# Retention with its output feature-major, its steps between the next pair's projections, and TensorE in program order there

## The chip, the cores and the metric

One core of a Trainium2 chip runs the kernel. The metric is the device time of one execution in microseconds (us); three runs of the kernel before took 2668.18, 2663.58 and 2665.60 us, median 2665.6. A core has five engines with queues of their own: TensorE (PE, with its weight loads PEld), VectorE (DVE), ScalarE (ACT), GpSimd (POOL) and SyncE (SP), which issues most transfers.

## The reference

A backbone of two layers over 512 latent and 256 context tokens of width 1024, in float32. Each layer normalizes and modulates the tokens, projects them (`h @ w_in`) to queries, keys, values and gates, mixes tokens in three branches (window attention, a Fourier transform, retention), sums the branches by gates, projects, and runs 32 experts of which each token uses two. The change concerns retention, 8 heads of 64, chunks of 128 tokens, both directions:

```python
inner = jnp.einsum('bcihd,bcjhd->bchij', qc, kc) * dec[None, None]
o_inner = jnp.einsum('bchij,bcjhe->bcihe', inner, vc)
u = jnp.einsum('bcjhd,jh,bcjhe->bchde', kc, zeta, vc)
# s_prev: a scan over the chunks, s = g_chunk * s + u_c
o_cross = jnp.einsum('bcihd,ih,bchde->bcihe', qc, xi, s_prev)

def retention_out(o, g):                      # o: both directions' sum
    mu = jnp.mean(o, axis=-1, keepdims=True)
    var = jnp.mean(jnp.square(o - mu), axis=-1, keepdims=True)
    on = ((o - mu) * lax.rsqrt(var + GN_EPS)).reshape(B, T, RET_WIDTH)
    return (jax.nn.silu(g.astype(F32)) * on).astype(g.dtype)
```

## The kernel before, in words

The layers run one after the other; layer 0 computes latent and context tokens (6 tiles of 128), layer 1 writes the latent ones alone (4 tiles). `h` lies feature-major, each value split in a high and a low part. `proj` (L267) makes 128 features of all tokens: SyncE loads two tiles of weights `raw`, ScalarE and VectorE split them into `hl` (L237, L238), and TensorE does 24 matmuls of 512 moving columns for the latent tokens and 24 of 256 for the context (L275 to L277), into PSUM tiles `mm`. In layer 0 each `proj` ends with a step of the modulation of what comes later (`ada_step`: a 1 MB transfer `wada`, four matmuls L149 into the tile `ov`, VectorE's add L199).

Retention goes by pairs of heads p = 0 to 3. `ret_proj` makes k and q (each rotated by `rot`: VectorE L286, L287, GpSimd L288, L289), v (transposed to token-major `vtok` by `to_tokens`, L296) and the gate `sgr`. `ret_chain` makes token-major keys `ktok` (L296), values times decay (L444), q times decay (GpSimd, L438), the states (L452, then a recursion on VectorE), the inner products of keys and queries (L473, times the mask L475), and then the output of a tile of 128 tokens in token-major order, 64 features per head: L482 takes the masked products as stationary operand and v as moving one, L487 q as stationary and the state as moving one, 64 moving columns both. Mean, centred value and variance are VectorE reductions over the 64 features (L498 to L507) and ScalarE's square (L503), the inverse root is a power on GpSimd (L142), GpSimd multiplies (L509), TensorE transposes to feature-major (L514), and VectorE multiplies by the gate (L517) and splits (L243).

A scheduler chooses the order of each engine's instructions from the program, so retention's matmuls of a pair lie between those of the next pair's projections, or of the first of attention behind pair 3. PSUM tiles come from pools that set who waits: three banks `mm`, two `sc`, two `tr` (transposes), one `ov`. A stationary operand of type float32 takes two records of matmul in the trace.

Of the kernel before, what the change touches and what calls it, by code (L numbers as in the profile page):

```python
# [15 lines left out]
OP = mybir.AluOpType  # L16
# [18 lines left out]
T1_MASK, T1_KA, T1_VA = 0, 384, 1152  # L35
T2_LAT, T2_CTX, T2_CF, T2_ALT, T2_ALTC, T2_ROW, T2_ROWC, T2_N = 0, 1024, 1280, 1536, 1540, 1542, 1799, 1928
CP, _o = {}, 0
for _k, _n in (("ident", 128), ("tri", 128), ("iota1", 64), ("iota0", 32), ("i64", 16), ("kcon", 96), ("tok2", 6),
               ("hbm2", 2), ("zc", 2)):
    CP[_k] = (_o, _o + _n)  # L40
    _o += _n
# [19 lines left out]
def tile_backbone(ctx: ExitStack, tc: tile.TileContext, a: dict, out: bass.AP, stop=None, dbg=None):  # L61
# [51 lines left out]
    # DRAM scratch  # L113
# [6 lines left out]
    cin = const(16, "cin", a["c"])  # L120
    cp = const(480, "cp")
# [7 lines left out]
    tok2, hbm2, zc = (cp[:, CP[k][0]:CP[k][1]] for k in ("tok2", "hbm2", "zc"))  # L129
# [39 lines left out]
    def ada_feature(l, row):  # L169
        """sh1 and norm*(1+sc1), one value for each partition: [128, stream, kc]"""  # L170
# [21 lines left out]
    def ada_steps():  # L192
# [10 lines left out]
        # the last: over a partition's rows on DVE, over the partitions on PE (one stream, the latent one)  # L203
# [42 lines left out]
    def make_h(l, xt_l, xt_c):  # L246
        """xt_*: token-major tiles, already times rstd"""
# [70 lines left out]
    decay = {}  # L318

    def decay_logs(l):  # L320
# [13 lines left out]
        Z = cst.tile([128, 16], F32, name=f"Z{l}", tag="Z")      # [h of f | h of b]  # L334
# [26 lines left out]
    # =====================================================================  # L361
    def layer(l, xt_l, xt_c):
# [10 lines left out]
        rope, t1 = unit("rope"), unit("t1")  # L373
        SP.dma_start(rope, a["t1"][:, 0:2048])
        SP.dma_start(t1[:, 0:384], a["t1"][:, 2048:2432])
        CA, SA = rope[:, T1_CA:T1_CA + 512], rope[:, T1_SA:T1_SA + 512]
        CR, SR = rope[:, T1_CR:T1_CR + 512], rope[:, T1_SR:T1_SR + 512]
        mask = t1[:, T1_MASK:T1_MASK + 384]
# [10 lines left out]
        def o_tiles(b):  # L389
            """[high, low][group] of a branch's output, feature-major"""  # L390
# [10 lines left out]
        def ret_proj(p):  # L401
# [3 lines left out]
            sgr = rv[:, 768:1536]  # L405
            pc, pl = proj(l, p * 4, both)
# [10 lines left out]
            to_tokens(vtok, lambda i: (vc[:, i * 128:i * 128 + 128] if i < 2 else vl[:, (i - 2) * 128:(i - 1) * 128]),  # L417
                      ((0, 2), (2, 4)))
# [4 lines left out]
            return k, q, vtok, sgr  # L423

        def ret_chain(p, st):
            k, q, vtok, sgr = st
# [3 lines left out]
            vz = rb[:, 0:1536].rearrange("p (t h d e) -> p t h d e", t=6, h=2, d=2)  # L430
            St = rc[:, 0:768].rearrange("p (t d e) -> p t d e", t=6, d=2)
            ktok = rc[:, 768:1536].rearrange("p (t c) -> p t c", t=6)
            to_tokens(ktok, lambda i: k[:, i * 128:i * 128 + 128], ((0, 2), (2, 4)))
            # q times xi, for the states' part
            qs = slice(0, 768) if full else lsl
            nt = 6 if full else 4
            for d in range(2):
# [3 lines left out]
            for h in range(2):  # L441
                for d in range(2):
                    j = d * 8 + p * 2 + h
                    DVE.tensor_scalar(vz[:, :, h, d, :], vtok[:, :, h * 64:h * 64 + 64], Z[:, j:j + 1], None, op0=OP.mult)  # L444
            # states
            g_f, g_b = g128[:, p * 2:p * 2 + 1], g128[:, p * 2 + 1:p * 2 + 2]
            u = []
            for lo, n in ((0, 2), (2, 4)):
                up = pso()
                for i in range(n):  # L450
                    for h in range(2):
                        PE.matmul(up[h * 64:h * 64 + 64, i * 128:i * 128 + 128], ktok[:, lo + i, h * 64:h * 64 + 64],  # L452
                                  vz[:, lo + i, h, :, :], start=True, stop=True, skip_group_check=True)
# [12 lines left out]
            # inner products  # L466
            for lo, n in (((0, 2), (2, 4)) if full else ((2, 4),)):
                sc = [pss(), pss()]
                for i in range(n):
                    ts = slice((lo + i) * 128, (lo + i) * 128 + 128)  # L470
                    for h in range(2):
                        hs = slice(h * 64, h * 64 + 64)
                        PE.matmul(sc[h][:, i * 128:i * 128 + 128], k[hs, ts], q[hs, ts], start=True, stop=True)  # L473
                for h in range(2):
                    DVE.tensor_tensor(SD[:, h, lo:lo + n, :], sc[h][:, 0:n * 128].rearrange("p (t i) -> p t i", t=n),  # L475
                                      bmid(Dt[:, p * 2 + h, :], n), op=OP.mult)
            oo = [pss(), pss()]
            for t in TL:
                ts = slice(t * 128, t * 128 + 128)
# [909 lines left out]
```

## Time and profile before

| | |
|---|---|
| median of three runs | 2665.6 us |
| span of the profiled execution (first to last instruction) | 2652.4 us |
| mean granted clock of TensorE | 0.945 of full speed |
| TensorE busy | 2404.5 us, 91% |
| VectorE, ScalarE, GpSimd busy | 1045.9, 571.0, 469.6 us |
| moved by DMA | 594 MB, 224 GB/s on average |

The profiled execution's own time is its span with what lies around it at start and end; against the runs' median that is 13 us. A row of the timeline gives the start of a merged group of instructions, its busy time, the engine and line, the tiles written and read, their shape and number, and in brackets the idle time before it with what ended it. "PEclk" is the granted clock of TensorE over a stretch, 1.00 being 2.4 GHz. `sc`, `tr`, `ov` and `mm` are PSUM tiles; `ra` holds k and q, `rv` v and the gate, `rb` products and output, `rc` states and keys, `rq` q times decay.

### The profile page before, as it was taken

To read this page: it belongs to the slowest core of one execution; us is meant where nothing else is said; L and a number is where in the kernel's file an instruction comes from. 1 tells how busy PE (TensorE), PEld (TensorE's weight loads), DVE (VectorE), ACT (ScalarE), POOL (GpSimd) and SP (SyncE) were. 2 spreads that over 40 slices of the span, in tenths; PEclk is the share of its full clock that TensorE was granted. 3 is DMA by queue.
4 is the path that set the end of the run, shared out by engine and by line. 5 is a ranking of instruction groups with operands and counts; after the bars stand their busy time and mean duration, and the time that the engine had idled before them with its cause. 6 is when DMAs were issued, how large, how long until landed. Compare 5 with 4: busy or idle time off the path is not lost. (4 is left out here: it accounts for less than half of the span.)

```text
span 2652.4 us, 44021 instructions
## 1 busy us (share of the span) xinstructions
PE 2404.5 (91%) x17245; PEld 1580.7 (60%) x17245; DVE 1045.9 (39%) x3181; ACT 571.0 (22%) x1285; POOL 469.6 (18%) x414
## 2 busy tenths in 40 slices
PE   5999999999999979999999599999999898997774
PEld 3777766688889944434443388766888743343221
DVE  5434445635234643233332644565335521221112
ACT  3211134521223211011110422245224200000000
POOL 0212110000222412111211123210022321121111
PEclk8988889999999979999999799999999899998897
DMA  7423211235225389899999621110235599999996
GB/s 273 162 96 108 102 51 63 81 111 209 71 64 179 138 331 417 352 371 389 415 417 411 237 72 46 58 48 21 88 97 173 207 379 417 411 410 407 416 415 253
DMA packets 129730, 594.43 MB, mean 224 GB/s; under 512 B 20940, under 2 KB 22052, under 8 KB 73968
## 3 DMA queue, kind: packets, MB, share of 16 engines
q1 hardware_dynamic: 115184, 561.92, 55.0%
q0 software_dynamic: 13376, 26.27, 2.6%
q8 instruction: 138, 2.26, 0.3%
q10 hardware_dynamic: 960, 3.39, 0.3%
q14 instruction: 72, 0.59, 0.1%
HBM read 579.74 MB, written 28.25 MB: 229 GB/s over the span
## 5 line engine op out<-in xcount | busy, mean ns | idle before, releaser
L1079 PE MATMUL mm<-w_gu,xT 128*32 128x256 f32 (+1 forms) x3776 | 564.4, 505 | 85.1 <-DMA w_gu<-in_w_gu_dram 81.7
L1079 PEld LDWEIGHTS mm<-w_gu,xT 128*32 128x32 f32 (+1 forms) x3776 | 192.0, 127 | 390.8 <-issue 227.4
L275 PE MATMUL mm<-hH,hl 128*128 128x512 f32 x800 | 319.7, 401 | 1.7 <-DVE shuf L287 0.9
L276 PE MATMUL mm<-hL,hl 128*128 128x512 f32 x800 | 316.1, 395 | 0.0
L277 PE MATMUL mm<-hH,hl 128*128 128x512 f32 x800 | 315.5, 395 | 0.4 <-DVE hl L238 0.4
L238 DVE TENSOR_TENSOR hl<-raw,hl 128x512 fp32r<-128x512 f32 x248 | 183.3, 741 | 252.1 <-ACT hl L237 251.8
L1104 PE MATMUL mm<-w_d,aT 128*32 128x256 f32 (+1 forms) x1888 | 267.0, 488 | 6.9 <-DVE aT L1094 5.9
L237 ACT CAST hl<-raw 128x512 fp32r<-128x512 f32 x248 | 153.4, 620 | 385.9 <-PE mm L277 250.6
L1084 ACT ACTIVATE act<-mm 128x256 f32<-128x256 f32 (+1 forms) x87 | 30.1, 346 | 899.0 <-PE mm L1079 865.0
L1113 POOL DMA_INDIRECT y_d<-y,gd x87 | 87.7, 1008 | 742.3 <-DVE y L1112 562.3
L1104 PEld LDWEIGHTS mm<-w_d,aT 128*32 128x32 f32 (+1 forms) x1888 | 90.6, 124 | 157.0 <-issue 124.0
L1085 DVE TENSOR_TENSOR act<-act,mm 128x256 f32<-128x256 f32 (+1 forms) x87 | 32.2, 370 | 380.3 <-ACT act L1084 380.3
L275 PEld LDWEIGHTS mm<-hH,hl 128*128 128x128 f32 x800 | 151.3, 189 | 41.1 <-issue 6.1
L277 PEld LDWEIGHTS mm<-hH,hl 128*128 128x128 f32 x800 | 151.3, 189 | 35.5 <-issue 3.9
L276 PEld LDWEIGHTS mm<-hL,hl 128*128 128x128 f32 x800 | 151.2, 189 | 32.4 <-issue 5.2
L275 PE MATMUL mm<-hcH,hl 128*128 128x256 f32 x480 | 143.8, 300 | 5.8 <-ACT ra L408 3.9
L276 PE MATMUL mm<-hcL,hl 128*128 128x256 f32 x480 | 141.8, 295 | 0.0
L277 PE MATMUL mm<-hcH,hl 128*128 128x256 f32 x480 | 141.5, 295 | 0.0
L986 POOL DMA_INDIRECT xg<-h_d,gd x87 | 91.1, 1047 | 148.1 <-issue 71.2
L275 PEld LDWEIGHTS mm<-hcH,hl 128*128 128x128 f32 x480 | 96.2, 200 | 19.0 <-issue 5.7
L276 PEld LDWEIGHTS mm<-hcL,hl 128*128 128x128 f32 x480 | 96.4, 201 | 4.9 <-issue 1.2
L277 PEld LDWEIGHTS mm<-hcH,hl 128*128 128x128 f32 x480 | 96.5, 201 | 3.6 <-issue 3.1
(385 smaller groups left out, 3694.4 us busy)
## 6 DMA issues: line engine op xcount, KB each, us to landing
w_gu<-in_w_gu_dram SPq DMA_DIRECT2D x256, 1024.0 KB
w_d<-in_w_d_dram SPq DMA_DIRECT2D x128, 1024.0 KB
raw<-in_w_in_dram SPq DMA_DIRECT2D x200, 256.0 KB
wada<-in_w_ada_dram SPq DMA_DIRECT2D x48, 1024.0 KB
raw<-in_w_br_dram SPq DMA_DIRECT2D x48, 256.0 KB
yb<-y_d SPq DMA_DIRECT2D x10, 1024.0 KB
raw<-in_w_out_dram SPq DMA_DIRECT2D x32, 256.0 KB
h_d<-hb POOLq DMA_DIRECT2D x10, 512.0 KB, 6.4
```

The lines of the kernel that those rows point to most:

```text
L237: ACT.copy(hl[:, 0], r)
L238: DVE.tensor_tensor(hl[:, 1], r, hl[:, 0].bitcast(F32), op=OP.subtract)
L275: PE.matmul(o[:, 0:n], wh, h[kc], start=kc == 0, stop=False)
L276: PE.matmul(o[:, 0:n], wh, lo[kc], start=False, stop=False)
L277: PE.matmul(o[:, 0:n], wl, h[kc], start=False, stop=kc == 7)
L986: POOL.indirect_dma_start(out=xg, out_offset=None, in_=h2_d[l].rearrange("r (a c) -> (r a) c", c=sz * 8), in_offset=bass.IndirectOffsetOnA ...
L1079: PE.matmul(p1[q * sz:q * sz + sz, 0:n], xT[:, k * sz:k * sz + sz], w[:, q * n:q * n + n], start=k == 0, stop=k == 7, skip_group_check=True)
L1084: ACT.activation(sv, pv[:, :, 0, :], AF.Silu)
L1085: DVE.tensor_tensor(sv, sv, pv[:, :, 1, :], op=OP.mult)
L1104: PE.matmul(p2[q * sz:q * sz + sz, 0:n], aT[:, j * 128 + q_ * sz:j * 128 + q_ * sz + sz], w[:, q * n:q * n + n], start=k == 0, stop=k == 3 ...
L1113: s = POOL.indirect_dma_start(out=y_d[l].rearrange("r (a c) -> (r a) c", c=n), out_offset=bass.IndirectOffsetOnAxis(ap=di, axis=0), in_=y, ...
```

## The change

The output is made feature-major. v is taken to token-major order not by a transpose but by a matmul with a 128 x 128 table, the identity less the mean over a head (`cenm`), so that v, and with it every sum of v's, has mean zero over a head. The output products swap their operands: L500 has v (64 columns of a head) as stationary operand and the masked products as moving one, L509 the state (64 x 64) as stationary operand and q as moving one; both have 128 moving columns, and the two heads lie on the two halves of the partitions of one bank. ScalarE squares the result (L516) and copies it (L517), GpSimd multiplies the copy by the gate (L518), TensorE sums the squares over a head with a table of two columns (`bo`, L522), VectorE adds epsilon, GpSimd takes the power, ScalarE spreads the 12 values over 768 columns (L527), TensorE transposes that (L532), and VectorE multiplies and splits (L534). VectorE's reductions and subtractions of before are gone. The states' first product goes to a bank `tr`, its values times decay to tiles of their own.

`ret_chain` has five steps. Step 1 (`ktok`, q and v times decay, inner products of the latent tiles) stands behind the next pair's k projection, step 2 (states, inner products of the context tiles) behind its q, step 3 (L500, L509 and the copies) behind v, step 4 (L522 to L527) behind the gate and v's table matmuls, step 5 (L532, L534) behind the k projection of the pair after that, ahead of that chain's step 1. For pair 3 the projections are attention's k, v and first q. Within `manual_schedule` TensorE's instructions are issued in this order. In layer 0 a projection's ada step stands ahead of the step.

```diff
-    def to_tokens(dst, src, segs):
+    def to_tokens(dst, src, segs, by=None):
...
-                PE.transpose(t[:, i * 128:i * 128 + 128], src(lo + i), ident)
+                if by is None:
+                    PE.transpose(t[:, i * 128:i * 128 + 128], src(lo + i), ident)
+                else:
+                    PE.matmul(t[:, i * 128:i * 128 + 128], src(lo + i), by, start=True, stop=True)
             ACT.copy(dst[:, lo:lo + n, :], t[:, 0:n * 128].rearrange("p (i c) -> p i c", i=n))
...
-            to_tokens(vtok, lambda i: (vc[:, i * 128:i * 128 + 128] if i < 2 else vl[:, (i - 2) * 128:(i - 1) * 128]),
-                      ((0, 2), (2, 4)))
+            yield
             for (o, seg) in zip(proj(l, p * 4 + 3, qsegs), ([csl, lsl] if full else [lsl])):
...
+            to_tokens(vtok, lambda i: (vc[:, i * 128:i * 128 + 128] if i < 2 else vl[:, (i - 2) * 128:(i - 1) * 128]),
+                      ((0, 2), (2, 4)), cenm)
+            yield
...
         def ret_chain(p, st):
...
+            segs = ((2, 4), (0, 2)) if full else ((2, 4),)
+
+            def inner(lo, n):
+                sc = [pss(), pss()]
...
+                        PE.matmul(sc[h][:, i * 128:i * 128 + 128], k[hs, ts], q[hs, ts], start=True, stop=True)
+                for h in range(2):
+                    DVE.tensor_tensor(SD[:, h, lo:lo + n, :], sc[h][:, 0:n * 128].rearrange("p (t i) -> p t i", t=n),
+                                      bmid(Dt[:, p * 2 + h, :], n), op=OP.mult)
+
+            zb = Z.rearrange("p (d h) -> p h d", d=2)[:, p * 2:p * 2 + 2, :]
+            to_tokens(ktok, lambda i: k[:, i * 128:i * 128 + 128], ((0, 2), (2, 4)))
+            for t in range(6):
+                vt = vtok[:, t].rearrange("p (h e) -> p h e", h=2).unsqueeze(2).broadcast_to([128, 2, 2, 64])
+                DVE.tensor_tensor(vz[t], vt, blast(zb, 64), op=OP.mult)
             for d in range(2):
                 POOL.tensor_tensor(qx[:, d, qs].rearrange("p (t i) -> p t i", t=nt),
...
+            inner(*segs[0])
+            yield
...
-                up = pso()
+                up = pst() if lo == 0 else pso()
...
+            if full:
+                inner(*segs[1])
+            yield
+
+            oo = {lo: pss() for lo, n in segs}
+            for lo, n in segs:
                 for i in range(n):
                     for h in range(2):
                         hs = slice(h * 64, h * 64 + 64)
+                        PE.matmul(oo[lo][hs, i * 128:i * 128 + 128], vtok[:, lo + i, hs], SD[:, h, lo + i, :],
+                                  start=i == 0, stop=False, skip_group_check=True)
+            for lo, n in segs:
+                for i in range(n):
+                    t = lo + i
+                    dirs = [d for d in range(2) if (t, d) not in ((0, 0), (1, 1))]
+                    for d in dirs:
+                        for h in range(2):
+                            hs = slice(h * 64, h * 64 + 64)
+                            PE.matmul(oo[lo][hs, i * 128:i * 128 + 128], St[hs, t, d, :],
+                                      qx[hs, d, t * 128:t * 128 + 128],
+                                      start=False, stop=d == dirs[-1], skip_group_check=True)
+
+            cen, sq = rb[:, 0:768], rb[:, 768:1536]
+            for lo, n in segs:
+                cs_ = slice(lo * 128, (lo + n) * 128)
+                ACT.activation(sq[:, cs_], oo[lo][:, 0:n * 128], AF.Square)
+                ACT.copy(cen[:, cs_], oo[lo][:, 0:n * 128])
+            POOL.tensor_tensor(cen[:, qs], cen[:, qs], sgr[:, qs], op=OP.mult)
+            yield
+            vp = pso()
             for t in TL:
+                PE.matmul(vp[:, t * 2:t * 2 + 2], sq[:, t * 128:t * 128 + 128], bo, start=True, stop=True)
+            var = small(12, "var")
             t0 = TL[0]
-                DVE.tensor_reduce(mu3[:, :, h], ov, axis=AX.X, op=OP.add, negate=True)
...
-                DVE.tensor_tensor(cen[:, :, h, :], ov, blast(mu3[:, :, h], 64), op=OP.add)
-            ACT.activation(sq, cen, AF.Square)
...
-            DVE.tensor_reduce(v3, sq, axis=AX.X, op=OP.add)
...
-            POOL.tensor_tensor(cen, cen, blast(v3, 64), op=OP.mult)
...
+            DVE.tensor_scalar(var[:, t0 * 2:12], vp[:, t0 * 2:12], 1e-5, None, op0=OP.add)
+            rsqrt(var[:, t0 * 2:12], var[:, t0 * 2:12], 12 - t0 * 2)
+            ACT.copy(sq[:, qs].rearrange("p (n e) -> p n e", e=64), blast(var[:, t0 * 2:12], 64))
+            yield
+            for lo, n in segs:
                 t = pst()
                 for i in range(n):
-                    PE.transpose(t[:, i * 128:i * 128 + 128], cf[:, lo + i, :], ident)
+                    PE.transpose(t[:, i * 128:i * 128 + 128], sq[:, (lo + i) * 128:(lo + i) * 128 + 128], ident)
                 f = W2("rf", n * 128)
-                DVE.tensor_tensor(f, t[:, 0:n * 128], sgr[:, seg], op=OP.mult)
+                DVE.tensor_tensor(f, t[:, 0:n * 128], cen[:, lo * 128:(lo + n) * 128], op=OP.mult)
                 split_to(o_ap("R", 0, p, lo == 0), o_ap("R", 1, p, lo == 0), f)
...
+        with tc.manual_schedule(engines={ET.PE}):
+            done = None
+            for p in range(4):
+                nxt = []
+                if p == 3:
+                    sa = [unit("sa"), unit("sa")]
+                chain = ret_chain(p, st)
+                for _ in (ret_proj(p + 1, nxt) if p < 3 else kv()):
+                    if done is not None:
+                        next(done, None)
+                        done = None
+                    next(chain, None)
+                st, done = nxt, chain
+            for _ in done:
+                pass
         o_tiles("A")
...
+    half = np.kron(np.eye(2), np.full((64, 64), 1.0 / 64))
+    put("bo", half[:, ::64])
...
+    c["t1"] = np.ascontiguousarray(np.concatenate([CA, SA, CR, SR, mask, np.eye(128) - half], 1).astype(f))
```

Three places of TensorE's order in layer 0 follow (`ov` with `wada` is the ada step, `mm` a projection's tile). First, the output products of pair 0, before from the first of them on: L482 and L487 alternate by ones and twos (a row of these is one matmul, two records).

```order
L473 MATMUL sc_1119<-ra_449 128x128 x4
L482 MATMUL sc_1130<-rv_450,rb_1068 128x64
L487 MATMUL sc_1130<-rc_1069,rq_1067 128x64
L482 MATMUL sc_1130<-rv_450,rb_1068 128x64
L487 MATMUL sc_1130<-rc_1069,rq_1067 128x64
L482 MATMUL sc_1130<-rv_450,rb_1068 128x64
L487 MATMUL sc_1130<-rc_1069,rq_1067 128x64 x2
L482 MATMUL sc_1130<-rv_450,rb_1068 128x64
```

After, the same place:

```order
L149 MATMUL ov_1035<-wada_1036,cs 32x512 x4
L500 MATMUL sc_1047<-rb_837,rv_451 64x128 x8
L500 MATMUL sc_1048<-rb_837,rv_451 64x128 x4
L509 MATMUL sc_1047<-rq_836,rc_838 64x128 x16
L509 MATMUL sc_1048<-rq_836,rc_838 64x128 x4
L275 MATMUL mm_1097<-hH_279,hl_1088 128x512
```

All of L500 now stand together, then all of L509, behind an ada step and ahead of a projection's first matmul, and no row has 64 moving columns.

Second, pair 0's transposes (L514 before, L532 after) with what stands around them. Before:

```order
L277 MATMUL mm_1281<-hH_280,hl_1277 128x512
L473 MATMUL sc_1543<-ra_757 128x128 x2
L473 MATMUL sc_1544<-ra_757 128x128 x2
L514 MATMUL tr_1176<-cp,rb_1068 128x128 x2
L514 MATMUL tr_1183<-cp,rb_1068 128x128 x4
L275 MATMUL mm_1280<-hcH_283,hl_1272 128x256
```

After:

```order
L277 MATMUL mm_1197<-hcH_283,hl_1194 128x256
L149 MATMUL ov_1249<-wada_1250,cs 32x512 x4
L532 MATMUL tr_1263<-cp,rb_837 128x128 x4
L532 MATMUL tr_1272<-cp,rb_837 128x128 x2
L297 MATMUL tr_1282<-cp,ra_760 128x128 x2
L297 MATMUL tr_1286<-cp,ra_760 128x128 x4
L455 MATMUL sc_1300<-ra_760 128x128
L455 MATMUL sc_1301<-ra_760 128x128
```

Before, the transposes followed inner products of the next pair and stood in the midst of a projection; now they stand behind the whole k projection and its ada step, and the transposes of the next pair's keys (L297) follow at once, with four `tr` tiles in a row.

Third, the new matmuls of step 4, which have no counterpart before:

```order
L277 MATMUL mm_1096<-hcH_283,hl_1093 128x256
L149 MATMUL ov_1146<-wada_1147,cs 32x512 x4
L299 MATMUL tr_1164<-t_67_414,vc_1043 128x128 x2
L299 MATMUL tr_1168<-t_67_414,vl_1044 128x128 x4
L522 MATMUL ov_1174<-cp,rb_837 128x2 x6
L275 MATMUL mm_1198<-hH_279,hl_1189 128x512
```

The table matmuls of v (L299) and the six matmuls of two columns (L522) stand between an ada step and the next projection.

## Rows read from the trace of the kernel before

**Rows 1.** The page: span, and busy time, share and instructions of each engine.

```profile
span 2652.4 us, 44021 instructions
...
PE 2404.5 (91%) x17245; PEld 1580.7 (60%) x17245; DVE 1045.9 (39%) x3181; ACT 571.0 (22%) x1285; POOL 469.6 (18%) x414
```

**Rows 2.** Windows: stretch, length, engines' busy us (x instructions), clock, DMA, GB/s.

```profile
90.00:358.00 268.00, 260.54 (x1481) 205.07 (x1480) 103.17 (x206) 43.56 (x86) 52.50 (x32) 0.88 0.29 99
147.00:163.00 16.00, 16.00 (x75) 13.51 (x74) 1.16 (x2) 0.00 (x0) 0.00 (x0) 0.66 0.00 1
97.00:147.00 50.00, 50.00 (x310) 39.86 (x308) 19.81 (x39) 9.98 (x20) 9.22 (x6) 1.00 0.37 128
1545.00:1727.00 182.00, 174.89 (x1055) 144.95 (x1053) 82.66 (x180) 45.36 (x84) 44.52 (x32) 0.96 0.18 54
```

**Rows 3.** Timeline of TensorE, layer 0, pair 0: start, us, line, tiles, count, idle.

```profile
148.25 0.43 PE L482 MATMUL sc<-rv,rb 128*128 128x64 f32 x2
148.61 0.43 PE L487 MATMUL sc<-rc,rq 64*128 64x64 f32 x2
...
161.38 1.12 PE L487 MATMUL sc<-rc,rq 64*128 64x64 f32 x8
162.43 0.79 PE L277 MATMUL mm<-hH,hl 128*128 128x512 f32 x1
...
163.45 0.63 PE L276 MATMUL mm<-hL,hl 128*128 128x512 f32 x1
163.88 0.63 PE L277 MATMUL mm<-hH,hl 128*128 128x512 f32 x1
...
170.91 1.54 PE L514 MATMUL tr<-cp,rb 128*128 128x128 f32 x6 [4.47 <-POOL rb L509]
174.24 0.58 PE L275 MATMUL mm<-hcH,hl 128*128 128x256 f32 x1 [1.78 <-ACT ra L408]
```

**Rows 4.** Timeline of TensorE, layer 1, pair 0.

```profile
1582.63 0.39 PE L275 MATMUL mm<-hH,hl 128*128 128x512 f32 x1
1582.95 1.09 PE L452 MATMUL ov<-rb,rc 128*64 128x128 f32 x16
...
1588.44 0.33 PE L482 MATMUL sc<-rv,rb 128*128 128x64 f32 x2
...
1593.19 0.66 PE L487 MATMUL sc<-rc,rq 64*128 64x64 f32 x8
1593.78 0.50 PE L275 MATMUL mm<-hH,hl 128*128 128x512 f32 x1
1594.11 0.39 PE L276 MATMUL mm<-hL,hl 128*128 128x512 f32 x1
1594.34 0.40 PE L277 MATMUL mm<-hH,hl 128*128 128x512 f32 x1
...
1597.42 1.71 PE L473 MATMUL sc<-ra 64*128 64x128 f32 x16
```

**Rows 5.** Groups by line and form, TensorE, layer 0's stretch: busy, mean ns, idle.

```profile
L487 PE MATMUL sc<-rc,rq 64*128 64x64 f32 x160 | 34.2, 380 | 0.0
L482 PE MATMUL sc<-rv,rb 128*128 128x64 f32 x96 | 25.9, 374 | 0.0
```

**Rows 6.** Timeline of TensorE, transposes of k; layer 0's Fourier part.

```profile
129.66 0.82 PE L296 MATMUL tr<-cp,ra 128*128 128x128 f32 x6
...
504.99 0.50 PE L646 MATMUL sc<-t,fb 128*128 128x2 f32 x4
505.35 0.89 PE L649 MATMUL sc<-t,fb 128*128 128x256 f32 x3
```

**Rows 7.** Groups by line and form, VectorE and GpSimd, layer 0's stretch.

```profile
L199 DVE TENSOR_TENSOR arow<-ov,arow 128x512 f32<-128x512 f32 x17 | 11.7, 690 | 21.1 <-PE ov L149 21.1
...
L438 POOL TENSOR_TENSOR rq<-ra,misc 128x768 f32<-128x768 f32 x8 | 15.6, 1970 | 7.0 <-PE ov L149 7.0
...
L142 POOL TENSOR_TENSOR var<-var,mhalf 128x12 f32<-128x12 f32 x4 | 9.1, 2282 | 172.9 <-DVE var L507 172.9
```

More of the change, by code (lines that the diff above doesn't have):

```diff
@@ L405, in ret_proj @@
             sgr = rv[:, 768:1536]
+            st += [k, q, vtok, sgr]
             pc, pl = proj(l, p * 4, both)
@@ L477, in ret_chain @@
-            oo = [pss(), pss()]
-            for t in TL:
-                ts = slice(t * 128, t * 128 + 128)
-                dirs = [d for d in range(2) if (t, d) not in ((0, 0), (1, 1))]
-                for h in range(2):
-                    PE.matmul(oo[h][:, t * 64:t * 64 + 64], SD[:, h, t, :], vtok[:, t, h * 64:h * 64 + 64],
-                              start=True, stop=False, skip_group_check=True)
-                for d in dirs:
-                    for h in range(2):
-                        hs = slice(h * 64, h * 64 + 64)
-                        PE.matmul(oo[h][:, t * 64:t * 64 + 64], qx[hs, d, ts], St[hs, t, d, :],
-                                  start=False, stop=d == dirs[-1], skip_group_check=True)
@@ L490, in ret_chain @@
-            n = len(TL)
-            t0 = TL[0]
-            cen = rb[:, 0:768].rearrange("p (t h e) -> p t h e", t=6, h=2)[:, t0:6]
-            sq = rb[:, 768:1536].rearrange("p (t h e) -> p t h e", t=6, h=2)[:, t0:6]
-            mu = small(2 * n, "mu")
-            mu3 = mu.rearrange("p (t h) -> p t h", h=2)
-            for h in range(2):
-                ov = oo[h][:, t0 * 64:384].rearrange("p (t e) -> p t e", t=n)
-                DVE.tensor_reduce(mu3[:, :, h], ov, axis=AX.X, op=OP.add, negate=True)
@@ L499, in ret_chain @@
-            DVE.tensor_scalar(mu, mu, 1.0 / 64, None, op0=OP.mult)
-            for h in range(2):
-                ov = oo[h][:, t0 * 64:384].rearrange("p (t e) -> p t e", t=n)
-                DVE.tensor_tensor(cen[:, :, h, :], ov, blast(mu3[:, :, h], 64), op=OP.add)
-            ACT.activation(sq, cen, AF.Square)
-            var = small(2 * n, "var")
-            v3 = var.rearrange("p (t h) -> p t h", h=2)
-            DVE.tensor_reduce(v3, sq, axis=AX.X, op=OP.add)
-            DVE.tensor_scalar(var, var, 1.0 / 64, 1e-5, op0=OP.mult, op1=OP.add)
@@ L508, in ret_chain @@
-            rsqrt(var, var, 2 * n)
-            POOL.tensor_tensor(cen, cen, blast(v3, 64), op=OP.mult)
-            cf = rb[:, 0:768].rearrange("p (t c) -> p t c", t=6)
-            for lo, n in (((0, 2), (2, 4)) if full else ((2, 4),)):
+                        PE.matmul(oo[lo][hs, i * 128:i * 128 + 128], vtok[:, lo + i, hs], SD[:, h, lo + i, :],
+                                  start=i == 0, stop=False, skip_group_check=True)
+            for lo, n in segs:
+                for i in range(n):
+                    t = lo + i
+                    dirs = [d for d in range(2) if (t, d) not in ((0, 0), (1, 1))]
+                    for d in dirs:
+                        for h in range(2):
+                            hs = slice(h * 64, h * 64 + 64)
+                            PE.matmul(oo[lo][hs, i * 128:i * 128 + 128], St[hs, t, d, :],
+                                      qx[hs, d, t * 128:t * 128 + 128],
+                                      start=False, stop=d == dirs[-1], skip_group_check=True)
@@ L661, in fou, with kv @@
                 seg(fu[:, csl], 256, 512, 1280, T2_CTX, T2_ALTC, T2_ROWC, True)
-        o_tiles("R")
-        pr = ret_proj(0)
-        for p in range(4):
-            nxt = ret_proj(p + 1) if p < 3 else None
-            if p == 3:
-                pc, pl = proj(l, 16, both)
-                rot(ka[:, lsl], pl, CA, SA)
-                ACT.copy(ka[:, csl], pc)
-                pc, pl = proj(l, 17, both)
-                vc, vl = W2("vac", 256), W2("val")
-                ACT.copy(vc, pc)
-                ACT.copy(vl, pl)
-                to_tokens(va, lambda i: (vc[:, i * 128:i * 128 + 128] if i < 2 else vl[:, (i - 2) * 128:(i - 1) * 128]),
-                          ((0, 2), (2, 4)))
-                sa = [unit("sa"), unit("sa")]
-                att_q(0, sa)
-            ret_chain(p, pr)
-            pr = nxt
+        def kv():
+            pc, pl = proj(l, 16, both)
+            rot(ka[:, lsl], pl, CA, SA)
+            ACT.copy(ka[:, csl], pc)
+            yield
+            pc, pl = proj(l, 17, both)
+            vc, vl = W2("vac", 256), W2("val")
+            ACT.copy(vc, pc)
+            ACT.copy(vl, pl)
+            yield
+            to_tokens(va, lambda i: (vc[:, i * 128:i * 128 + 128] if i < 2 else vl[:, (i - 2) * 128:(i - 1) * 128]),
+                      ((0, 2), (2, 4)))
+            att_q(0, sa)
+            yield
+        o_tiles("R")
+        st = []
+        for _ in ret_proj(0, st):
+            pass
[13 more added lines that the diff above has]
+            for _ in done:
+                pass
         o_tiles("A")
```

39 lines of the change are left out of this document (14 added, 25 removed).

## The prediction

> **What bounds the kernel now.** I began with the page. TensorE is busy in 91% of the span, VectorE in 39%, ScalarE and GpSimd in about a fifth [rows 1]: what leaves TensorE's row of work shortens the kernel, unless a wait takes its place. Then the stretches. Layer 0's retention runs from the start of pair 1's projections (90) to its last output transposes (358), layer 1's from 1545 to 1727. TensorE is busy for 260.54 us of 268 and for 174.89 of 182, so idle time is 7.5 and 7.1 us, and the mean granted clock is 0.88 and 0.96 [rows 2]. The clock has two levels, 1.0 (2.4 GHz) and 0.5 (1.2 GHz), so 0.88 over 268 us means 0.12 x 268 / 0.5 = 64 us at the lower one, and 0.96 over 182 us 15 us. Where it falls is seen in two more stretches: projections alone (97 to 147) have 1.00, and the stretch after 147, which is full of work and opens with the two output lines L482 and L487, has 0.66 [rows 2]. The timeline of TensorE gives the prices: a 512-column projection matmul comes every 0.43 us at the lower clock, and behind the output stage TensorE stands still for 4.47 us and 1.78 us [rows 3]; in layer 1 one comes every 0.23 us at the upper clock (1594.11 to 1594.34) [rows 4].
>
> The stretch lies ahead of everything else of its layer, and outside it TensorE's and SyncE's orders stay. What TensorE saves here therefore moves the rest forward one for one; I find nothing later that holds a fixed time.
>
> **The output products.** In pair 0 of layer 0 they last from 148.25 to 162.43, 14.2 us [rows 3]. For all four pairs the two lines are busy 34.2 + 25.9 = 60.1 us [rows 5], and busy time counts overlapping ends: pair 0's 22 rows of the timeline, from 148.25 to 161.38, add up to 15.7 for its 14.2, so I take 0.9 x 60.1 = 54 us. In layer 1 a pair takes 1588.44 to 1593.78, 5.3 us, four of them 21 [rows 4]. Before: 75 us.
>
> After, the same number of matmuls stands there (records, of which each fp32 matmul has two: per pair 24 + 40 in layer 0, 16 + 32 in layer 1), in two blocks with 128 moving columns instead of 64. L500 has 64 stationary columns, its two heads on the two halves of the array's columns, as the states' line L452 of before: 16 records between 1582.95 and some 1584.05, 0.069 each [rows 4]. That is 160 records x 0.069 = 11 us. L509 has 64 rows and 64 columns, which no row has. From below L452's 0.069; L487's eight records take 0.59, 0.074 each, with half the moving columns. From above L473, two heads on 64 rows each with 128 moving columns: 16 in 1.71, 0.107 each [rows 4]; and, far above, the 0.18 at which L482 and L487 go when they alternate two by two in layer 0 (148.25 to 148.61 for two) [rows 3]. It shares rows' halving with one and columns' halving with the other, so I take the middle, 0.088: 288 records, 25 us. After: 36 us; **gain 39**, by the ends 45 and 13.
>
> A rule speaks against the lower end. The Trainium skill, TensorEngine Tiling (Array Packing), section Gotcha 1: PSUM Pressure, says that different row tiles cannot access the same PSUM bank at once. Before, the two heads of L487 wrote to two banks; now both heads of L509 write to one. By that rule L509 would go at 0.107 or above and the gain would be 34. No row of before has two row tiles in one bank.
>
> **The clock.** Of the 64 us at the lower level in layer 0, four output stages at 9 or 10 us take 37 and idle time 6; some 21 are projections, which save (0.43 - 0.23) / 0.43 = 46% [rows 3, 4], 10 us. In layer 1 I take 9 of the 15 us for such work, an estimate, and get 4. **Gain 14**, if the new blocks don't bring the clock down; nothing if they do.
>
> **Idle time.** 14.6 us is all of it. Most stands ahead of L514, which waits for VectorE's and GpSimd's normalization, and ahead of the projection behind [rows 3]. After, L522 and L532 stand one whole projection behind what they wait for, 24 x 0.23 + 24 x half that = 8 us. Their chain is an add, the power (2.28 us, twelve columns) and one broadcast copy; only where the q products (1.97 us each) or a rotation are ahead of the power on GpSimd [rows 7] can it come late, by a microsecond. **Gain 14.6** before new waits.
>
> **Fewer interruptions.** Counted in the program's order, TensorE changes between projections and other work 149 times in the two stretches before and 89 times after. Going in takes 0.32 instead of 0.23 (1582.63 to 1582.95) [rows 4]: 60 changes at 0.08, **gain 4.5**.
>
> **What is added.** The mean is taken off v by six fp32 matmuls instead of six transposes: 12 records x 0.107 + 0.2 = 1.5 us against 0.82 [rows 6], 0.6 more in 8 pairs, 5 us. The variance is six (layer 1: four) matmuls of two moving columns with a 128-column stationary: four such records take 0.36 [rows 6], so 12 x 0.09 and 8 x 0.09, with entering, 1.1 and 0.75; 7 us in all. **Cost 12.** VectorE loses two reductions, a scaling, two subtractions and another reduction a pair and gains an add; ScalarE gains two copies; all of it lies beside TensorE, which these engines lag only at the waits below. The new table is one 64 KB transfer, in the queue with the first tables, long before its use.
>
> **New waits.** In program order TensorE cannot step past a waiting instruction. Two I can name. First, behind each k projection step 5 of a pair stands right before step 1 of the next: L532 fills both transpose banks, and L297 must wait until VectorE's L534 has read the first. VectorE at that time may have the ada add (0.69 us) [rows 7] and a split of weights ahead; at about 0.7 us each with the multiply, two or three operations are 1.4 to 2.1 us, 2 in layer 0 (three times) and 0.8 in layer 1 without the ada step (three times). Second, L477 needs the one "ov" bank that the ada step's add empties: 0.6 us, four times. Sum 6 + 2.4 + 2.4, less 1 for what overlaps, rounded: **cost 10**, between 0 (VectorE always ahead) and 30 (another 0.6 us at each of some 32 steps). Behind the waiting instruction the next projection is queued, and for that nothing but TensorE itself waits.
>
> **Sum.** -39 - 14 - 14.6 - 4.5 + 12 + 10 = -50. The profiled execution's span is 2652.4; the three runs have a median of 2665.6, 13 us around the span, which the change does not touch. 2665.6 - 50.6 = **2615 us**.
>
> **Rivals.**
> 1. The clock falls again at the new stages (chance 0.17). For: before, it fell while TensorE did L482 and L487 without a gap [rows 2, 3], and L509 with a quarter of the array, then L522 with two columns, are work of that kind. Against: in layer 1 the projections right behind pair 0's output products still come every 0.23 us [rows 4]. Then the 14 are not had, and some 18 us of new blocks run at half speed, +10: 2665.6 - 26 = 2640.
> 2. Row tiles of one bank do not overlap, or their changes cost what alternation costs in layer 0 (0.10). At 0.18 a record L509 takes 52 instead of 25: 2642; by the skill's rule alone, at 0.107, 2620, within the forecast.
> 3. Slower (0.06). The fixed order is the mechanism: the scheduler of before filled waits with projection matmuls, and now each of 32 steps stands in front of the next projection. With the 60 us that are gained without new waits, the kernel ends slower once the mean wait of a step exceeds 1.9 us. At 2.3, a split, an ada add and a multiply on VectorE each time, it is 2665.6 - 60 + 74 = 2680. Against: of the five steps only one follows its producer directly; the others have a projection of 8 us between.
> 4. The gain stays in the stretch, since something later is bound by transfers that were started earlier and do not move (0.04): within 5 us of 2665.6. For: long parts of the page's DMA row are full. Against: those transfers wait for buffers that the same TensorE work frees.
> 5. More (0.08): L509 at 0.069 and no new waits: -39 - 6 and no 10, 2599; with an earlier start of layer 1's first attention steps perhaps 2590.
>
> The forecast itself has 0.55, its own range 2600 to 2632. What a measurement can tell from no change is 0.2%, about 5 us. Rivals 1, 2 and 5 are faster too, so faster has 0.55 + 0.17 + 0.10 + 0.08 = 0.90, same 0.04, slower 0.06. The range for 8 in 10 leaves out part of the slow end and of the gains beyond 75: 2588 to 2646.
>
> **What would show it.** Right: L500 with L509 at most 6 us a pair in layer 0, mean clock of the stretch 0.97 or more, its length 90 to some 325; L297 with an idle time of 1 to 2 us behind k projections, waiting for VectorE. Wrong: stretches at 0.5 behind the new blocks (rival 1), L509 above 0.15 a record (2), idle time of over 2 us ahead of most steps (3), or a stretch that is 50 us shorter in a kernel that is not (4).

## The result and the profile after

The changed kernel takes 2597.28 us (median of four runs, 2592.6 to 2601.29) against 2664.59 for the kernel before, ratio 0.9755 [0.9732, 0.9778]. That is 65 us faster by the ratio, 67 by the medians; the forecast was 51, at 2615, with the range 2588 to 2646. The time lies in that range and 3 us below the forecast's own one, 2600 to 2632. Beside the experiments it was timed again: 0.9745 [0.9732, 0.9759].

The page of the changed kernel, against [rows 1]:

```profile
span 2590.7 us, 44254 instructions
...
PE 2354.7 (91%) x17373; PEld 1546.0 (60%) x17373; DVE 1038.1 (40%) x3149; ACT 581.7 (22%) x1309; POOL 472.3 (18%) x414
```

The spans differ by 61.7 us. This execution has 2 us around its span. If the one before had as little, the 13 us that the prediction put around that span were mostly the spread between executions.

To compare the stretches, both kernels are cut at the same work: in layer 0 from 90 us, near the start of pair 1's projections, to attention's first product with v, in layer 1 from the end of layer 0's experts to the same place. Windows, columns as in [rows 2], of the kernel before:

```profile
90.00:369.00 279.00, 270.77 (x1524) 211.53 (x1522) 111.20 (x233) 48.51 (x96) 55.14 (x34) 0.88 0.28 96
1476.00:1738.00 262.00, 227.15 (x1292) 184.95 (x1290) 141.90 (x324) 78.72 (x147) 65.00 (x45) 0.90 0.27 90
```

and of the changed kernel:

```profile
90.00:322.00 232.00, 224.39 (x1606) 180.21 (x1607) 108.56 (x221) 57.62 (x119) 57.27 (x34) 0.99 0.34 119
1431.00:1675.00 244.00, 214.10 (x1344) 174.65 (x1344) 135.30 (x303) 82.89 (x155) 65.81 (x45) 0.94 0.30 98
```

Layer 0's stretch is 47 us shorter and its clock went from 0.88 to 0.99; layer 1's is 18 us shorter. The rest of the kernel takes the same within a few us, so nothing was given back later.

Adding up in both traces the time from each TensorE record's start to the next one's, over these stretches (idle time apart), gives the balance, us (the last column is the change in time):

| | before | after | forecast and measured |
|---|---|---|---|
| output products | 54.1 + 20.4 | 15.2 + 11.7 | -39, measured -48 |
| projections and ada steps | 351.7 | 331.7 | -18.5 (clock and interruptions), measured -20 |
| inner products | 18.3 | 12.4 | 0, measured -6 |
| transposes, v's table matmuls, variance | 26.9 | 44.3 | +12, measured +17 |
| TensorE idle | 25.6 | 20.6 | -14.6 + 10, measured -5 |
| the rest: states, attention's first products | 26.5 | 22.9 | 0, measured -4 |
| of all but idle: at the lower clock | 91 | 17 | |

At the start of layer 1's stretch, ahead of retention, lie some 10 us of either idle sum, and 10 of the 17 us at the lower clock; the change hardly touched either.

Where the products stood [rows 3], the changed kernel's timeline of TensorE, pair 0 of layer 0, has two dense blocks:

```profile
125.44 1.53 PE L500 MATMUL sc<-rb,rv 128*64 128x128 f32 x24
126.90 2.40 PE L509 MATMUL sc<-rq,rc 64*64 64x128 f32 x40
129.23 0.50 PE L275 MATMUL mm<-hH,hl 128*128 128x512 f32 x1
```

3.8 us instead of 14.2: 0.061 us a record for L500 and 0.058 for L509. The place of the first named wait, behind a k projection:

```profile
151.09 0.88 PE L532 MATMUL tr<-cp,rb 128*128 128x128 f32 x6
154.03 1.05 PE L297 MATMUL tr<-cp,ra 128*128 128x128 f32 x6 [2.06 <-DVE rf L534]
155.01 1.94 PE L455 MATMUL sc<-ra 64*128 64x128 f32 x16
156.88 0.79 PE L275 MATMUL mm<-hH,hl 128*128 128x512 f32 x1
157.48 0.63 PE L276 MATMUL mm<-hL,hl 128*128 128x512 f32 x1
157.90 0.63 PE L277 MATMUL mm<-hH,hl 128*128 128x512 f32 x1
158.33 0.53 PE L275 MATMUL mm<-hH,hl 128*128 128x512 f32 x1
158.69 0.40 PE L276 MATMUL mm<-hL,hl 128*128 128x512 f32 x1
```

TensorE waits 2.06 us for VectorE's L534, and behind that wait it runs at the lower clock for some 3.4 us (512-column matmuls 0.43 apart, then 0.23). Groups of the changed kernel, layer 0's stretch, columns as in [rows 5]:

```profile
L509 PE MATMUL sc<-rq,rc 64*64 64x128 f32 x160 | 9.6, 272 | 0.0
L455 PE MATMUL sc<-ra 64*128 64x128 f32 x96 | 8.6, 319 | 0.0
L500 PE MATMUL sc<-rb,rv 128*64 128x128 f32 x96 | 6.1, 277 | 0.0
L522 PE MATMUL ov<-cp,rb 128*128 128x2 f32 x48 | 5.8, 249 | 0.0
...
L297 PE MATMUL tr<-cp,ra 128*128 128x128 f32 x24 | 3.9, 288 | 6.3 <-DVE rf L534 6.3
...
L477 PE MATMUL ov<-rb,rc 128*64 128x128 f32 x32 | 2.6, 282 | 1.3 <-DVE arow L199 1.3
```

Both waits that the prediction named are there, at the places it named: 6.3 us in three waits (forecast 6) and 1.3 in four (forecast 2.4). In layer 1 (total us, times, longest):

```profile
PE tr L297 <- DVE rf L534: 1.3, 1, 1.3
PE tr L297 <- ACT rc L300: 1.0, 2, 0.6
```

That is 2.3 us (forecast 2.4), of which 1.0 waited for ScalarE's copies and not for VectorE. All together they make 9.9 us, forecast 10.

### The profile page after: what moved, and what is told of

Same layout as the page of the kernel before. It is cut to its first block, busy times and chain, and to the rows that moved or that the text cites. A ratio compares the mean times of both kernels' runs of the same rounds, so it can differ in the third digit from the quotient of the medians.

```text
span 2590.7 us, 44254 instructions
## 1 busy us (share of the span) xinstructions
PE 2354.7 (91%) x17373; PEld 1546.0 (60%) x17373; DVE 1038.1 (40%) x3149; ACT 581.7 (22%) x1309; POOL 472.3 (18%) x414
## 5 line engine op out<-in xcount | busy, mean ns | idle before, releaser
L1112 PE MATMUL mm<-w_gu,xT 128*32 128x256 f32 (+1 forms) x3776 | 571.9, 508 | 70.8 <-DMA w_gu<-in_w_gu_dram 66.8
L277 PEld LDWEIGHTS mm<-hH,hl 128*128 128x128 f32 x800 | 150.7, 188 | 36.1 <-issue 3.6
L275 PE MATMUL mm<-hcH,hl 128*128 128x256 f32 x480 | 138.7, 289 | 2.4 <-DVE m L583 1.0
L277 PE MATMUL mm<-hcH,hl 128*128 128x256 f32 x480 | 137.0, 285 | 0.0
L275 PEld LDWEIGHTS mm<-hcH,hl 128*128 128x128 f32 x480 | 92.1, 192 | 11.2 <-issue 1.9
L288 POOL TENSOR_TENSOR shuf<-shuf,rope 128x512 f32<-128x512 f32 x26 | 35.8, 1380 | 328.0 <-DVE shuf L287 199.2
```

Source lines behind the costliest of these rows:

```text
L275: PE.matmul(o[:, 0:n], wh, h[kc], start=kc == 0, stop=False)
L277: PE.matmul(o[:, 0:n], wl, h[kc], start=False, stop=kc == 7)
L288: POOL.tensor_tensor(s, s, sin, op=OP.mult)
L1112: PE.matmul(p1[q * sz:q * sz + sz, 0:n], xT[:, k * sz:k * sz + sz], w[:, q * n:q * n + n], start=k == 0, stop=k == 7, skip_group_check=True)
```

## The experiments

Each has its ratio to the kernel before on the same chip. Products and idle time are read as in the table above.

**The form alone, the order alone.** Three runs take the change apart. Without the fixed order, the steps in their places:

```diff
-        with tc.manual_schedule(engines={ET.PE}):
+        if True:
```

> The changed kernel without the fixed program order: the scheduler places TensorE's instructions again. Theory S (the gain is in the form of the output products and in the clock that they leave alone): the gain stays, 2590 to 2612 us; the waits of L297 behind L534 (6.3 us in layer 0 of the changed kernel) are filled with projections, but the waits of new chains may be longer. Rival O (the order and the places of the steps make the gain): 2625 us or more, with TensorE idle or at half clock again in the retention stretches.

Measured: 2585.76 us, 0.9736 [0.9719, 0.9752], theory S, a little below its range; no time at the lower clock and no idle time in layer 0's stretch:

```profile
90.00:311.50 221.50, 221.50 (x1596) 178.13 (x1588) 105.86 (x220) 57.98 (x119) 58.66 (x34) 1.00 0.36 124
```

The fixed order is not what makes the gain; the scheduler fills the places of its two-microsecond waits.

The feature-major output alone, each chain in one piece:

```diff
                 for _ in (ret_proj(p + 1, nxt) if p < 3 else kv()):
-                    if done is not None:
...
+                    pass
+                for _ in chain:
+                    pass
```

(also without the fixed order)

> The feature-major output alone: each pair's chain is written in one piece behind the next pair's projections, as before, and the scheduler places it. Theory S: output products near 27 us instead of 74, most half-clock time gone, 2600 to 2625 us. Rival O: the chain stands in a lump again, its waits are on the path, 2640 us or more.

Measured: 2593.38, 0.9771 [0.975, 0.9793], theory S, below its range; products 15.7 + 12.0, lower clock 7 us in layer 0 and 16 in layer 1. Against the run above, with the steps placed, some 9 us are lost; the intervals just touch. This run and the next keep the change's smaller edits (the states' bank, own tiles for values times decay, the latent tiles first); what those are worth alone was not run.

The steps and the fixed order alone: token-major products, mean and variance on VectorE, as in the kernel before.

```diff
-            oo = {lo: pss() for lo, n in segs}
...
+            oo = [pss(), pss()]
+            for t in TL:
+                for h in range(2):
+                    PE.matmul(oo[h][:, t * 64:t * 64 + 64], SD[:, h, t, :], vtok[:, t, h * 64:h * 64 + 64],
...
```

> The steps and the fixed program order alone: the output stays token-major (64 moving columns, mean and variance on VectorE as before, all of them in step 3, transposes in step 5, v transposed). Theory S: the output products still take some 70 us and the clock still falls in them; only idle time ahead of the transposes (some 8 us) and some changes between kinds of work are saved: 2640 to 2665 us. Rival O: 2625 us or less.

Measured: 2607.21, 0.9809 [0.9792, 0.9825]. The time is in rival O's range: 51 us came without the new form, and theory S's 2640 to 2665 missed. But the form alone gained 61 us in the run above, so either brings most of the gain. Its products take 31.3 + 19.1 us. The timeline of that run, pair 0 of layer 0:

```profile
124.18 0.66 PE L500 MATMUL sc<-rv,rb 128*128 128x64 f32 x4
124.77 0.44 PE L505 MATMUL sc<-rc,rq 64*128 64x64 f32 x4
...
126.68 0.66 PE L505 MATMUL sc<-rc,rq 64*128 64x64 f32 x8
127.28 0.97 PE L500 MATMUL sc<-rv,rb 128*128 128x64 f32 x4
...
132.36 1.12 PE L505 MATMUL sc<-rc,rq 64*128 64x64 f32 x8
133.41 0.79 PE L275 MATMUL mm<-hH,hl 128*128 128x512 f32 x1
```

Eight records of the state product take 0.60 us (126.68 to 127.28), as in layer 1 before [rows 4], while in layer 0 before two took 0.36 [rows 3]. In program order the two heads stand side by side; the scheduler before had put layer 0's products head by head. The clock still falls within the block, with no gap ahead of it.

A part of the gain from 54 us to 31 is the clock's. Of the 54 us of layer 0's products before, 37 were at the lower clock, of these 31 only 11, of the new form's 15 none. Two records that took 0.36 us at the upper clock [rows 3] take 0.62 at the lower one, in the kernel before:

```profile
154.55 0.69 PE L482 MATMUL sc<-rv,rb 128*128 128x64 f32 x2
155.17 0.69 PE L487 MATMUL sc<-rc,rq 64*128 64x64 f32 x2
```

By these prices, an estimate, 16 of the 54 us and 5 of the 31 are the clock's: of the 23 us that the order saved, half come from the order of the records and half from less time at the lower clock. In layer 1, where the products were at the upper clock almost throughout, the order alone brings them from 20.4 to 19.1 us, the form from there to 11.7.

**Head by head, or kind by kind.** Two edits of the kernel before. First, L482 of all tiles ahead of L487 of all tiles:

```diff
             for t in TL:
...
+                              start=t == TL[0], stop=False, skip_group_check=True)
+            for t in TL:
...
                 for d in dirs:
```

> The kernel before with one edit: of each pair's output products all of the first kind (v moving) come first, then all of the second (state moving), instead of alternating by tiles; sizes, operands and the scheduler stay. Theory A (alternation costs: each change between full-height and half-height stationary operands is paid): the products of layer 0 fall from 54 us to 30 or less, and the clock falls later or not at all: 2625 to 2650 us. Theory W (it is the 64 moving columns): a record still takes 0.11 to 0.15 us, clock and time stay: 2655 to 2668 us.

Measured: 2632.77, 0.9906 [0.9889, 0.9923], products 36.1 + 15.0: the time is theory A's, the time of a record in layer 0 theory W's. The scheduler kept head after head, for the inner products L473 too:

```profile
147.69 1.16 PE L473 MATMUL sc<-ra 64*128 64x128 f32 x8
148.77 1.55 PE L480 MATMUL sc<-rv,rb 128*128 128x64 f32 x12
150.25 2.00 PE L488 MATMUL sc<-rc,rq 64*128 64x64 f32 x16
152.18 2.11 PE L480 MATMUL sc<-rv,rb 128*128 128x64 f32 x12
```

Without the changes between forms, a state record still takes 1.93 / 16 = 0.12, against 0.075 with the heads side by side, and an inner product's 1.08 / 8 = 0.135. The trace has the reason: head by head the records start one by one, 0.11 us apart; with the heads side by side (L505 of the run above, L509 and L455 of the changed kernel) they start in twos, at most 0.02 us apart, and the next two 0.11 us later.

Second, the two lines as they are, but in program order, heads side by side:

```diff
+            with tc.manual_schedule(engines={ET.PE}):
+                for t in TL:
...
```

> The kernel before with one edit: the output products (L482, L487) of a pair are issued in program order, that is by tiles of tokens with both heads side by side; everything else stays with the scheduler, sizes and operands stay. In layer 0 the scheduler had put them head by head, changing between L482 and L487 after every one or two. Theory H (half of layer 0's 54 us came of that order, not of the 64 moving columns): products of layer 0 about 31 us as in the run with the order alone, less half-clock time, total 20 to 35 us below before, 0.987 to 0.992. Theory W (width): products stay near 50 us, total within 8 us of before.

Measured: 2650.56, 0.9949 [0.9932, 0.9966]. The products came near what theory H said, 33.1 us in layer 0, 16 of them at the lower clock, but the time fell by only 14 and not by 20 to 35: layer 0's idle time went from 8 to 17 us, ahead of what follows the products. In that run's timeline:

```profile
158.76 1.65 PE L473 MATMUL sc<-ra 64*128 64x128 f32 x8 [2.00 <-DVE rb L503]
...
165.18 1.54 PE L515 MATMUL tr<-cp,rb 128*128 128x128 f32 x6 [4.76 <-POOL rb L510]
```

**The moving columns.** In the changed kernel each L500 and L509 was cut into two of 64 moving columns:

```diff
-                        PE.matmul(oo[lo][hs, i * 128:i * 128 + 128], vtok[:, lo + i, hs], SD[:, h, lo + i, :],
+                        for c in (0, 64):
+                            PE.matmul(oo[lo][hs, i * 128 + c:i * 128 + c + 64], vtok[:, lo + i, hs],
+                                      SD[:, h, lo + i, c:c + 64],
...
```

> The changed kernel with each output matmul (L500, L509) cut into two of 64 moving columns: twice the matmuls, same operands, bank and order. Theory V (a record's time is set by its form and fixed costs, about 0.06 us, more than by its columns): the products take 48 to 55 us instead of 27, ratio 0.983 to 0.987. Rival N (time goes with the columns): products stay near 27 to 32 us, ratio 0.975 to 0.978. If the clock falls with 64 columns, half-clock time appears in the stretch behind the products, and the time is another 10 to 20 us up.

Measured: 2607.17, 0.9797 [0.9782, 0.9812]. Timeline of that run:

```profile
125.78 1.67 PE L501 MATMUL sc<-rb,rv 128*64 128x64 f32 x48
127.38 2.60 PE L512 MATMUL sc<-rq,rc 64*64 64x64 f32 x80
129.90 0.50 PE L275 MATMUL mm<-hH,hl 128*128 128x512 f32 x1
```

Theory V is refuted: a record of 64 columns takes 0.032 us, and the products only 29.3 instead of 26.9 (rival N's range; the ratio lies above its 0.978). So the width alone was not what made the old products slow; the 128-column stationary operand, the order of heads and the changes of form are left. For the first the traces have rows: behind a 128-column stationary operand, records head by head start 0.11 us apart with 64 moving columns (L488 above) as with 128 (L473), and two heads' records with 64 (L505) take 0.11 too; behind a 64-column one two heads' records take 0.11 with 128 moving columns (L509) and 0.06 with 64 (L512). The clock does not fall in these blocks. The total is 10 us above the changed kernel timed beside it; the stretches' lengths explain 5 of that, the rest is open.

**Changes of form.** On top of the swap that stands last in this section, L500 and L509 alternate tile by tile:

```diff
             for lo, n in segs:
                 for i in range(n):
+                    t = lo + i
...
-            for lo, n in segs:
-                for i in range(n):
-                    t = lo + i
                     dirs = [d for d in range(2) if (t, d) not in ((0, 0), (1, 1))]
```

> The kernel with step 1 ahead of step 5, and the new output products alternating by tiles of tokens (L500 for both heads, then L509 for both heads, tile after tile) instead of two blocks: same matmuls, operands and banks. Theory A (a change between the two array forms costs some 0.1 us whatever the operands): 12 more changes a pair in layer 0 and 6 in layer 1, the products go from 27 to 33 us or more, 0.971 to 0.973. Rival B (in the old order the cost was the 128-column stationary operands and the head-by-head order, not the change): products 27 to 29 us, same ratio within 2 us.

Measured: 2585.57, 0.9729 [0.9714, 0.9744], against 0.9702 for its base on the same chip; products 21.1 + 15.3, 9.5 more. Timeline:

```profile
124.75 0.44 PE L501 MATMUL sc<-rb,rv 128*64 128x128 f32 x4
125.12 0.65 PE L507 MATMUL sc<-rq,rc 64*64 64x128 f32 x8
125.70 0.44 PE L501 MATMUL sc<-rb,rv 128*64 128x128 f32 x4
...
129.67 0.44 PE L507 MATMUL sc<-rq,rc 64*64 64x128 f32 x4
130.03 0.50 PE L275 MATMUL mm<-hH,hl 128*128 128x512 f32 x1
```

The pair takes 5.28 us (124.75 to 130.03) instead of 3.79, with 10 changes more: 0.15 us a change, theory A.

**Two heads in one bank.** In layer 1 alone each head's products got a bank:

```diff
-            oo = {lo: pss() for lo, n in segs}
+            oo = {lo: [pss()] * 2 if full else [pss(), pss()] for lo, n in segs}
...
-                        PE.matmul(oo[lo][hs, i * 128:i * 128 + 128], vtok[:, lo + i, hs], SD[:, h, lo + i, :],
+                        PE.matmul(oo[lo][h][hs, i * 128:i * 128 + 128], vtok[:, lo + i, hs], SD[:, h, lo + i, :],
...
```

> The changed kernel with the two heads of the output products in two PSUM banks in layer 1 alone (layer 0 has no free bank; ScalarE then reads the halves in four operations of 64 partitions instead of two of 128). Theory X (two row tiles of one bank go at once, as one block's 0.058 us a record suggests): L509 in layer 1 stays at 0.056 to 0.062 us a record. Rival Y (they stand in each other's way in one bank): 0.03 to 0.05 us a record.

Measured, in one run: 2587.18 us, which by itself says nothing of the time. Pair 0 of layer 1, in that run and then in the changed kernel:

```profile
1521.67 1.09 PE L500 MATMUL sc<-rb,rv 128*64 128x128 f32 x16
1522.70 1.96 PE L509 MATMUL sc<-rq,rc 64*64 64x128 f32 x32
```

```profile
1525.73 1.09 PE L500 MATMUL sc<-rb,rv 128*64 128x128 f32 x16
1526.75 1.96 PE L509 MATMUL sc<-rq,rc 64*64 64x128 f32 x32
```

The same, so theory X; in both, the two heads' records start in twos.

**A better version.** The new pair's step 1 ahead of the old pair's step 5:

```diff
+                    next(chain, None)
                     if done is not None:
                         next(done, None)
                         done = None
-                    next(chain, None)
```

Beside it ran the changed kernel again.

> The changed kernel once more, beside the runs that follow on the same chip: its ratio to the kernel before, 0.9755 in its first runs, should be 0.974 to 0.977.

> The changed kernel with one edit: behind each k projection the new pair's step 1 (key transposes, inner products) stands ahead of the old pair's step 5 (L532, L534), so that the key transposes do not wait for VectorE's L534. Theory P (the waits of 6.3 us in layer 0 and 2.3 in layer 1, and the half clock behind them, are all that the fixed order costs against the scheduler): those waits go, half-clock time in layer 0's stretch goes from 7 us to about 0, and the time is 6 to 11 us below the changed kernel's, ratio 0.9715 to 0.9735. Rival Q (the wait moves to the next user of the transpose banks, L532 behind ScalarE's copies, and costs the same): within 3 us of the changed kernel.

Measured: 2597.09, 0.9745 [0.9732, 0.9759] for the changed kernel, 2583.58, 0.9694 [0.9681, 0.9708] for the edit, 13.5 us less and a little more than theory P gave. The same place of the timeline, and layer 0's stretch:

```profile
152.23 0.88 PE L297 MATMUL tr<-cp,ra 128*128 128x128 f32 x6
153.04 1.16 PE L455 MATMUL sc<-ra 64*128 64x128 f32 x16
154.13 0.88 PE L532 MATMUL tr<-cp,rb 128*128 128x128 f32 x6
```

```profile
90.00:312.00 222.00, 220.72 (x1608) 178.26 (x1608) 111.12 (x220) 58.12 (x120) 58.08 (x34) 1.00 0.36 124
```

The 2 us wait is gone, and with it the lower clock: L455 takes 1.09 us instead of 1.87. The stretch is 10 us shorter. Timed again, and with the scheduler in place of the fixed order (the edit of the first run):

> The kernel with step 1 ahead of step 5 once more, beside the runs that follow on the same chip: 0.968 to 0.971 of the kernel before.

> The same kernel without the fixed program order: the scheduler places TensorE's instructions. Theory P (once no step waits, the order has nothing left to give or to take): the same time within 4 us, TensorE idle in layer 0's retention stretch 0 to 1.5 us. Rival O (the fixed order is worth something of its own, as fewer changes between kinds of work): 4 us or more slower.

Measured: 2576.98, 0.9702 [0.9689, 0.9716], and 2576.18, 0.9691 [0.9678, 0.9704]. The same: once L297 waits no more, the fixed order has nothing left to give or to take. This kernel, with or without the fixed order, is the fastest version. One difference stays open: the run with the scheduler and without the swap stood at 0.9736 on another chip, though in its trace layer 0's and layer 1's stretches are as long as here (221.6 and 242.0 us, against 220.8 and 241.9). No trace explains it, so ratios from different chips are compared here to half a per cent only.

## Why the prediction was right, and where its sizes were not

Direction, range and mechanism held: the gain came in the two stretches, from products, clock and interruptions, and stayed. The terms were off by up to 9 us each, in both directions, so that the forecast fell 14 to 17 us short. Point by point:

- **The output products** were mis-sized, 39 instead of 48, and the reason given was partly wrong. L509 was put between 0.069 and 0.107 and taken at 0.088; it takes 0.058, below the lower end. The upper end, L473, was no fair neighbour: of the sixteen records of that row [rows 4] ten start one by one, 0.11 us apart, and only six in twos. L455, the same matmul with the heads in turn, takes 1.09 / 16 = 0.068. The step that failed is the bound from rows of another order. What made the old products slow in layer 0 was their order there (head by head, a change of form after every one or two), the lower clock that came with them, and their form: the order alone takes them from 54 to 31 us, half of that by the clock, the new form from there to 15. In layer 1 it was the form almost alone.
- **The rule of the Trainium skill** (TensorEngine Tiling (Array Packing), section Gotcha 1: PSUM Pressure) that spoke against this is not borne out for this form: two heads on two halves of rows and columns, which write to different partitions, start in twos and go at the same 0.058 to 0.059 in one bank as in two.
- **Clock and interruptions**, 18.5: 20 measured. The clock no longer falls at the products, and since the run with the order alone, in the same program order, still has it fall there and the one with the form alone does not, that is the form's doing. What the prediction did not see is that it falls behind the new waits, in layer 0 for 3.4 us after two of the three in this trace.
- **Idle time and new waits**: -14.6 + 10 against -5 measured. Both named waits are there, 9.9 us; at the other steps there is almost nothing.
- **What is added**, 12: 17 measured, of which 1.4 are v's matmuls of pair 0, which only the later window holds. Key transposes, 2.7 dearer, were left out, variance and v's table cost 1 to 1.5 more each, and the output transposes 1.4 less.
- **Inner products**: 6 us of gain were not in the sum. The printed order shows both heads in turn (L455 on two tiles), where the scheduler had put head after head (L473, four matmuls on one tile); it was not read as a price.
- **Rivals.** The new stages did not bring the clock down (1), banks do not matter (2), the waits of the 32 steps are 0.3 us on average, not 1.9 (3), nothing was kept from the end (4). The time is that of rival 5, 2599 at a chance of 0.08, but not for its reasons: L509 fell below its lower end, yet the new waits were there in full. That both come to the same time is luck: the inner products, which the sum left out, and the larger gain of the output products make up for the waits.
- **Form and order overlap.** The prediction added up terms as if each were tied to one part of the change. Form alone gives 61 us of 65, order and places alone 51: either takes the products out of the slow order and shortens the time at the lower clock (in layer 0 from 61 us to 7 and to 41, idle time apart).

## What to carry to other kernels

Where matmuls on half the rows or columns come in pairs, keep the two halves in turn and one form together: 0.068 against 0.135 us a record for the halves, 0.15 us for each change of form. Fewer moving columns shortened a record here only behind a 64-column stationary operand. Before fixing an order, look at which of its steps use the same PSUM banks back to back: a 2 us wait cost the clock behind it too, and a swap of two neighbours was worth 13 us here. And test form and order one by one, since their gains may be the same gain.

## What the runs showed of the hardware that was not expected

A fp32 record with a 64 x 64 stationary operand and 64 moving columns takes 0.032 us when two heads take turns, 0.058 with 128 columns; the two heads' records start together, in one bank as in two. Behind a 128-column stationary operand of 64 rows two heads' records take 0.11 us even with 64 moving columns. The granted clock fell within full TensorE work of the token-major products (in the order-alone run 3 us into pair 0's block and 6 into pair 1's, with no idle time ahead), in none of the feature-major blocks, alternating or not, and it fell behind waits of 2 us. Why the token-major form brings it down is open: layer 1's first block before, of 5 us and in the same form, did not.
